# Residual of the late tokens turned by VectorE, and sums of their first norm taken along columns of a second copy of the input

## The chip, the cores and the metric

The kernel runs on one core of one Trainium2 chip. Its engines work side by side, each through its own queue, in order: TensorE (PE; its weight loads are shown apart as PEld), VectorE (DVE), ScalarE (ACT), GpSimd (POOL), and SyncE (SP), which only issues DMAs here. The time is that of the device in microseconds; for the kernel before it is the median of three runs. TensorE writes its results to PSUM, which has eight banks of 128 x 512 values; all other tiles lie in SBUF, 128 partitions wide.

## The reference

Two layers over 1024 tokens of 1024 features, float32: a retention layer with four heads, and a stick-breaking attention layer with eight heads whose keys and values come from the stream after the first layer. Each is normed before and after; `h` is the residual. Cut to what the change touches:

```python
def rms_norm(x, g):
    xf = x.astype(jnp.float32)
    y = xf * lax.rsqrt(jnp.mean(xf * xf, axis=-1, keepdims=True) + EPS)
    return (y * g.astype(jnp.float32)).astype(x.dtype)

h = x
u = rms_norm(h, ret_norm_pre[i])          # the first norm
proj = u @ ret_w_in[i]
...                                       # retention, gate, y = o @ ret_w_out[i]
h = h + rms_norm(y, ret_norm_post[i])     # the residual that is kept for the end
...                                       # shared keys and values, attention, gate
y = o @ sb_w_out[j]
h = h + rms_norm(y, sb_norm_post[j])      # the output
```

## The kernel before

Tokens are worked in two halves, 0 to 511 (early) and 512 to 1023 (late). Activations lie feature by feature: a tile has 128 features on the partitions and 512 tokens along the row, so the input is given transposed (`xT`). A float32 product is made of three faster ones: `split` (L511) writes each operand as a high part (ScalarE, L514, or L517 with a scale) and a low part (VectorE, L515 or L518), and `mm3` (L410) issues three matmuls, L413, L414 and L415. Weights come in loads of 256 KB (`wraw`) and are split into `whl`. Nearly all DMAs are issued by the helper at L360 on SP's queue.

**The first norm.** `a_open` has two halves. For the early tokens (`F`) the raw input is multiplied at once and scaled afterwards; its squares are added up by `squares` (ScalarE L557 and L560, VectorE L561), `rstd_col` sums over the partitions with four small matmuls against ones (L488), VectorE and GpSimd make the reciprocal root (L490, L492), `diag` spreads the column over a diagonal tile `sgn` (L499, L500), and `keep_row` broadcasts it with two matmuls (L506) into a row tile `acc` (ScalarE L508). `norm` (L588) then multiplies the input with that row and splits it into `xh` tiles. For the late tokens (`L`) `later` loads eight tiles of 128 x 512 into `v` and squares them in the same way, feature by feature; the same three steps (`stats1`) make their row, and `scale` (L605) applies it.

**The end.** The late tokens' output is made token by token: `finish` multiplies with the heads' outputs as the fixed operand, so that a tile has 128 tokens on the partitions. `prep` loads the last weights (`whl`, `ko`, `A`), the four tiles of residual `h` of 128 features-by-twos x 1024 (`xh`, 512 KB each) and the gain (`sgn`). Four blocks of 128 tokens follow; each has two or three pieces of twelve matmuls (`piece`, PSUM tags `ma` and `mb`), whose result VectorE adds up (L1387), ScalarE squares (L1388) and VectorE multiplies with the gain (L1393). The residual lies feature by feature, so `turn` (L1395) turns its 128 x 128 blocks with TensorE, eight for each block of tokens, into two PSUM tiles (`z` or `o`); `write` scales and adds it (L1406) and stores.

**What sets the order.** The program is written out step by step, with tables that hang steps onto chunks of matmuls (`at[j]`) and `merge` that spreads side steps over main ones. Then `arrange` (L101) plans anew: from a cost for each instruction and the dependencies it places every instruction of every engine, SP's DMAs among them, and fixes each queue's order. Tiles of one tag share a number of buffers (`BUFS`: `xh` 8, `ko` 2, `vo` 4, `wraw` 6, `whl` 3), and the plan keeps the order in which they are handed out.

Of the kernel before, what the change touches and what calls it, by code (L numbers as in the profile page):

```python
# [307 lines left out]
@with_exitstack  # L308
def trunk(ctx, tc, xT, wts, gains, trig, ident_in, cols, last_gain, out):

# [213 lines left out]
    turned = out[0:512, :].rearrange("a (b t) -> (a b) t", b=2)  # L524
    straight = out[512:1024, :]
    st_d = [[dr.tile([128, 512], F32, tag=f"st{h}{d}", name=f"st{h}{d}") for d in range(2)] for h in range(NH)]
    y_d = [[dr.tile([128, 512], F32, tag=f"y{t}{c}", name=f"y{t}{c}") for c in range(8)] for t in range(2)]
# [20 lines left out]
    def a_open():  # L548
# [26 lines left out]
        def stats(box):  # L575
            def stat1():
                box.col = rstd_col(box.acc)

            def stat2():
                box.d = diag(box.col)  # L580

            def stat3():
                box.row = keep_row(box.d)
            return [stat1, stat2, stat3]
# [9 lines left out]
        def later(k):  # L594
            i, c = k // 2, k % 2
            if c == 0:
                F.kept[i] = S("v", [2, 512])
            src = F.kept[i][:, c]
            dma(src, xT[128 * (i + 4 * c):128 * (i + 4 * c) + 128, HT:2 * HT])
            squares(L, src, k)  # L600

        def scale(kt):
# [4 lines left out]
        return F, [lambda k=k: load(k) for k in range(8)], stats(F), [lambda k=k: norm(k) for k in (0, 1, 2, 3, 4, 5, 6, 7)], \  # L607
            [lambda k=k: later(k) for k in range(8)], stats(L), scale

# [722 lines left out]
    def c_post(t, y_d, acc):  # L1332
# [23 lines left out]
        return [stat1, stat2, row] + in_turn(8, 1, load, add)  # L1356

    def finish(t, P, ys):

        w, hs, box = {}, [], {}  # L1360

        def prep(u):
# [7 lines left out]
            a = S("xh", [1024])  # L1370
            dma(a[:], h_d[t][u][:])
            hs.append(a)
# [21 lines left out]

        def turn(b):  # L1395
            box["h", b] = [PS("o" if b % 2 else "z") for _ in range(2)]
            for c in range(8):
                nc.tensor.transpose(box["h", b][c // 4][:, 128 * (c % 4):128 * (c % 4) + 128],
                                    hs[c // 2][:, 512 * (c % 2) + 128 * b:512 * (c % 2) + 128 * b + 128], ident[:])

        def write(b):
            r, y = S("col", [4]), box["y"]
            G.tensor_tensor(r[:, 0:1], box["s"][:, 3:4], mhalf[:, 0:1], ALU.pow)
            for nh in range(2):
                cl = slice(512 * nh, 512 * nh + 512)
                V.scalar_tensor_tensor(y[:, cl], y[:, cl], r[:, 0:1], box["h", b][nh][:], ALU.mult, ALU.add)  # L1406
                dma(straight[128 * b:128 * b + 128, cl], y[:, cl], nc.scalar if nh else nc.sync)

        def last():
            for b in range(4):  # L1410
                piece(b, 0, 0, 512)
                if b < 3:
                    turn(b)
                for k, a in ((1, 512),) if b < 3 else ((1, 512), (2, 768)):
                    piece(b, k, a, 512 if b < 3 else 256)
                if b == 3:
                    turn(b)
                write(b)
# [58 lines left out]
    def layer_a():  # L1477
# [27 lines left out]
        for j, k in zip((8, 8, 9, 9, 10, 10, 11, 11), range(8)):  # L1505
            at[j].append(later[k])
        for j, k in zip((12, 13, 14), range(3)):
            at[j].append(stats1[k])
# [43 lines left out]
    def layer_c(units, out, load, kept, post):  # L1552
# [38 lines left out]
        filler = P.pieces(end, halt)  # L1591
        merge(heads[0].mix(0), (filler[:3], 0, 1))
        merge(rows_of(1), (filler[3:6], 0, 0))
        merge(heads[0].mix(1), (filler[6:], 0, 1), (rows_of(2), 0, 1))
        ys, acc = [], []
        for n in range(2, 16):
            A = heads[n // 2]
            if n % 2 == 0:
# [4 lines left out]
                pre[0]()  # L1603
            extra = []
            if n == 9:
# [86 lines left out]
```

## Time and profile before

| | us |
|---|---|
| median of 3 runs (1628.98 to 1630.21) | 1629.36 |
| the profiled execution | 1628.69 |
| its span, first to last instruction | 1626.7 |
| TensorE busy | 1619.3 |
| VectorE busy | 1219.1 |
| ScalarE busy | 804.1 |
| GpSimd busy | 122.1 |
| mean DMA rate | 238 GB/s |

The profiled execution takes 1.99 us more than its span. Rows of a timeline read: start, duration, engine, line and operation, the tile written and the tiles read without their numbers, the shape, and in brackets how long the engine had been idle and what released it. The chain of waits is followed back from the last instruction; its rows are start, duration, engine, tile and line. A matmul row lasts longer than the step to the next, since matmuls are pipelined: the step between starts is what one costs. A matmul of 128 x 1 in full float32 appears as two rows.

### The profile page before, as it was taken

To read this page: it belongs to the slowest core of one execution; us is meant where nothing else is said; L and a number is where in the kernel's file an instruction comes from. 1 tells how busy PE (TensorE), PEld (TensorE's weight loads), DVE (VectorE), ACT (ScalarE), POOL (GpSimd) and SP (SyncE) were. 2 spreads that over 40 slices of the span, in tenths; PEclk is the share of its full clock that TensorE was granted. 3 is DMA by queue.
4 is the path that set the end of the run, shared out by engine and by line. 5 is a ranking of instruction groups with operands and counts; after the bars stand their busy time and mean duration, and the time that the engine had idled before them with its cause. 6 is when DMAs were issued, how large, how long until landed. Compare 5 with 4: busy or idle time off the path is not lost.

```text
span 1626.7 us, 22505 instructions
## 1 busy us (share of the span) xinstructions
PE 1619.3 (100%) x7659; PEld 1351.5 (83%) x7659; DVE 1219.1 (75%) x1956; ACT 804.1 (49%) x1535; POOL 122.1 (8%) x271
## 2 busy tenths in 40 slices
PE   9999999999999999999999999999999999999998
PEld 7888888888888888888888888888888888888887
DVE  8997866654668888887689877767658666878775
ACT  8553334433456555544356665566544433554432
POOL 0000000000022212211000000000001111010010
PEclk9999999999999999999999999999999999999999
DMA  9556765543377878784776788978337877869781
GB/s 319 188 175 252 247 211 189 208 141 133 112 267 254 308 246 285 234 290 146 242 278 223 260 312 290 344 278 308 119 126 259 314 279 259 282 214 331 253 272 52
DMA packets 175890, 386.43 MB, mean 238 GB/s; under 512 B 18080, under 2 KB 34592, under 8 KB 173216
## 3 DMA queue, kind: packets, MB, share of 16 engines
q1 hardware_dynamic: 175056, 383.93, 68.3%
q8 instruction: 60, 0.98, 0.2%
q10 hardware_dynamic: 720, 1.07, 0.2%
q14 instruction: 54, 0.44, 0.1%
HBM read 263.82 MB, written 121.11 MB: 237 GB/s over the span
## 4 chain that ended last, share of the span: by engine, by line
PE 98%; DMA 1%; DVE 0%; issue 0%; ACT 0%; SPq 0%; DVEq 0%; POOLq 0%; POOL 0%
PE pma L413 12%; PE pma L415 12%; PE pma L414 12%; PE pmb L413 9%; PE pmb L415 9%; PE pmb L414 9%; PE po L414 6%; PE po L415 6%; PE po L413 6%; PE pz L414 3%; PE pz L415 3%; PE pz L413 3%; PE pz L1298 2%; PE pz L770 1%; PE pz L488 0%; DMA wraw<-in_wts_dram 0%
## 5 line engine op out<-in xcount | busy, mean ns | idle before, releaser
L514 ACT ACTIVATE whl<-wraw 128x512 fp32r<-128x512 f32 x266 | 156.2, 625 | 175.1 <-issue 62.6
L515 DVE TENSOR_TENSOR whl<-wraw,whl 128x512 fp32r<-128x512 f32 x266 | 176.1, 686 | 87.0 <-ACT whl L514 84.4
L1270 DVE TENSOR_TENSOR_SCAN sgn<-sgn 128x128 f32<-128x128 f32 (+3 forms) x64 | 86.6, 1352 | 17.3 <-POOL sgn L1268 17.3
L515 DVE TENSOR_TENSOR AT<-pz,AT 128x512 fp32r<-128x512 f32 (+1 forms) x96 | 51.1, 551 | 50.0 <-ACT AT L514 49.6
L514 ACT ACTIVATE AT<-pz 128x512 fp32r<-128x512 f32 (+1 forms) x96 | 45.1, 492 | 68.4 <-PE pz L1298 67.9
L413 PE MATMUL pmb<-oT,whl 128*128 128x512 f32 x192 | 75.9, 395 | 0.0
L415 PE MATMUL pmb<-oT,whl 128*128 128x512 f32 x192 | 75.3, 392 | 0.0
L414 PE MATMUL pmb<-oT,whl 128*128 128x512 f32 x192 | 75.1, 391 | 0.0
L413 PE MATMUL pmb<-qk,whl 128*128 128x512 f32 x184 | 72.5, 394 | 0.0
L415 PE MATMUL pmb<-qk,whl 128*128 128x512 f32 x184 | 72.1, 392 | 0.0
L414 PE MATMUL pmb<-qk,whl 128*128 128x512 f32 x184 | 71.8, 390 | 0.0
L515 DVE TENSOR_TENSOR whl<-vo,whl 128x512 fp32r<-128x512 f32 x62 | 41.7, 689 | 35.1 <-ACT whl L514 34.8
L884 ACT ACTIVATE f<-pma 128x512 f32<-128x512 f32 x52 | 30.7, 595 | 49.7 <-PE pma L415 49.3
L514 ACT ACTIVATE whl<-vo 128x512 fp32r<-128x512 f32 x62 | 37.5, 624 | 34.7 <-PE pma L415 17.5
L413 PE MATMUL pma<-xh,whl 128*128 128x512 f32 x136 | 53.3, 392 | 0.0
L414 PE MATMUL pma<-xh,whl 128*128 128x512 f32 x136 | 53.1, 390 | 0.0
L415 PE MATMUL pma<-xh,whl 128*128 128x512 f32 x136 | 53.1, 390 | 0.0
L1267 POOL TENSOR_SCALAR_AFFINE_SELECT A<-A 128x128 f32<-128x128 f32 x32 | 10.8, 336 | 535.1 <-DMA ko<-k 395.4
L907 ACT ACTIVATE wraw<-wraw,gn 128x256 f32<-128x256 f32 x102 | 45.4, 497 | 7.9 <-DMA wraw<-in_wts_dram 7.9
L1262 ACT ACTIVATE xh<-pz 128x512 f32<-128x512 f32 (+3 forms) x48 | 23.6, 492 | 48.6 <-PE pz L415 48.4
L1263 ACT ACTIVATE sgn<-pz 128x512 f32<-128x512 f32 (+2 forms) x96 | 46.7, 488 | 0.0
L1262 ACT ACTIVATE A<-pz 128x512 f32<-128x512 f32 (+3 forms) x48 | 23.6, 491 | 42.5 <-PE pz L415 42.4
(580 smaller groups left out, 5137.0 us busy)
## 6 DMA issues: line engine op xcount, KB each, us to landing
wraw<-in_wts_dram SPq DMA_DIRECT2D x332, 256.0 KB, 3.8
whl<-w SPq DMA_DIRECT2D x56, 512.0 KB, 6.0
vo<-in_wts_dram SPq DMA_DIRECT2D x70, 256.0 KB, 4.4
xh<-k SPq DMA_DIRECT2D x32, 512.0 KB, 6.8
v<-v SPq DMA_DIRECT2D x32, 512.0 KB, 5.0
k<-A SPq DMA_DIRECT2D x21, 512.0 KB, 4.9
e<-whl SPq DMA_DIRECT2D x10, 1024.0 KB, 6.7
whl<-e SPq DMA_DIRECT2D x10, 1024.0 KB, 6.7
```

The source lines that it names most:

```text
L413: MM(p, lh, rh, start=start, stop=False, **kw)
L414: MM(p, lh, rl, start=False, stop=False, **kw)
L415: MM(p, ll, rh, start=False, stop=stop, **kw)
L514: A_.activation(dst[0], src, AF.Copy)
L515: V.tensor_tensor(dst[1], src, f32(dst[0]), ALU.subtract)
L770: nc.tensor.transpose(pt[:, 128 * e:128 * e + 128], on[:, 128 * e:128 * e + 128], ident[:])
L884: A_.activation(c[:], p[:], AF.Copy)
L907: A_.activation(x, x, AF.Copy, scale=gcol(self.gains[col], 2 * (2 * i + k) + c))
L1262: A_.activation(a[:, o:o + ww], p[:, :ww], AF.Sigmoid)
L1263: A_.activation(n[:, o:o + ww], p[:, :ww], AF.Sigmoid, scale=-1.0)
L1270: V.tensor_tensor_scan(n[:, :W][:, ::-1], n[:, :W][:, ::-1], n[:, :W][:, ::-1], 1.0, ALU.mult, ALU.bypass)
L1298: nc.tensor.transpose(p[:, 128 * tb:128 * tb + 128], self.A[hh][tb][:, c0:c0 + 128], ident[:])
```

## The change

It has two parts, and the places in the tables that they need.

The residual of the late tokens is turned ahead of time. Eight steps `turn_h`, spread over four stages of the attention layer, each load one 128 x 512 tile of `h` into `vo`, let VectorE turn its blocks of 32 x 32 in place in the tile (a block (i, j) stays at (i, j), its inside is turned), and store it to `ht` in DRAM. `prep` then gathers each block of 128 tokens with four loads of 32 partitions, each made of 32 x 32 runs of 32 values (128 bytes), into `xh`, now with tokens on the partitions. `turn` is gone, and `write` reads `xh` instead of PSUM.

The late tokens' sum of squares is taken along rows of a second copy of the input, `x_late`, with tokens on the partitions: four loads of 512 KB into `ko`, each squared by ScalarE with its running sum (`accum_out`), which gives the column that the four small matmuls gave. `later` still loads the eight feature tiles, for `scale`, but squares nothing.

```diff
@@ trunk
+    ht_d = dr.tile([1024, 512], F32, tag="ht", name="ht")
@@ a_open
         def stats(box):
             def stat1():
-                box.col = rstd_col(box.acc)
+                if box is F:
+                    box.col = rstd_col(box.acc)
+                    return
+                ms = S("small", [4])
+                V.tensor_scalar(ms[:], box.sum[:], 1.0 / D, EPS, ALU.mult, ALU.add)
+                box.col = S("col", [4])
+                G.tensor_tensor(box.col[:], ms[:], mhalf[:, 0:4], ALU.pow)
...
             dma(src, xT[128 * (i + 4 * c):128 * (i + 4 * c) + 128, HT:2 * HT])
-            squares(L, src, k)
+
+        def sums(i):
+            if i == 0:
+                L.sum = S("small", [4])
+            w = S("ko", [1024])
+            dma(w[:], x_late[128 * i:128 * i + 128, :])
+            A_.activation(w[:], w[:], AF.Square, accum_out=L.sum[:, i:i + 1])
...
-            [lambda k=k: later(k) for k in range(8)], stats(L), scale
+            [lambda k=k: later(k) for k in range(8)], [lambda i=i: sums(i) for i in range(4)] + stats(L), scale
@@ before finish
+    def turn_h(k):
+        a, x = S("vo", [512]), S("vo", [512])
+        dma(a[:], h_d[1][k // 2][:, 512 * (k % 2):512 * (k % 2) + 512])
+        V.transpose(x[:], a[:])
+        dma(ht_d[128 * k:128 * k + 128, :], x[:])
+
@@ finish, prep
             a = S("xh", [1024])
-            dma(a[:], h_d[t][u][:])
+            for j in range(4):
+                dma(a[32 * j:32 * j + 32, :].rearrange("a (k b) -> a k b", b=32),
+                    ht_d[:].rearrange("(k a) t -> a k t", a=32)[:, :, 128 * u + 32 * j:128 * u + 32 * j + 32])
@@ finish
-        def turn(b):
-            box["h", b] = [PS("o" if b % 2 else "z") for _ in range(2)]
-            for c in range(8):
-                nc.tensor.transpose(box["h", b][c // 4][:, 128 * (c % 4):128 * (c % 4) + 128],
-                                    hs[c // 2][:, 512 * (c % 2) + 128 * b:512 * (c % 2) + 128 * b + 128], ident[:])
...
-                V.scalar_tensor_tensor(y[:, cl], y[:, cl], r[:, 0:1], box["h", b][nh][:], ALU.mult, ALU.add)
+                V.scalar_tensor_tensor(y[:, cl], y[:, cl], r[:, 0:1], hs[b][:, cl], ALU.mult, ALU.add)
...
-                if b < 3:
-                    turn(b)
...
-                if b == 3:
-                    turn(b)
@@ layer_a
-        for j, k in zip((12, 13, 14), range(3)):
+        for j, k in zip((11, 12, 13, 13, 14, 15, 15), range(7)):
             at[j].append(stats1[k])
@@ layer_c
-        merge(heads[0].mix(0), (filler[:3], 0, 1))
-        merge(rows_of(1), (filler[3:6], 0, 0))
+        merge(heads[0].mix(0), (filler[:2], 0, 1))
+        merge(rows_of(1), (filler[2:6], 0, 0))
...
-            extra = []
+            extra = [lambda k=k: turn_h(k) for k in (2 * n - 4, 2 * n - 3)] if 2 <= n < 6 else []
@@ inputs
+        "x_late": np.ascontiguousarray(x[0, HT:]),
```

The plan moves instructions; a number behind a name tells buffers apart and differs between the two programs. Lines from 580 on are some dozen higher in the changed kernel (L588 becomes L595, L1406 becomes L1421).

TensorE, the first block of the end, before (`qk` holds the last heads' outputs, `ko` and `A` the last weights):

```order
L413 MATMUL pma_15391<-ko_15293,qk_15160 128x512
L414 MATMUL pma_15391<-ko_15293,qk_15160 128x512
L415 MATMUL pma_15391<-ko_15293,qk_15160 128x512
L1398 MATMUL pz_15409<-ident,xh_15254 128x128 x2
L1398 MATMUL pz_15409<-ident,xh_15296 128x128 x2
L1398 MATMUL pz_15410<-ident,xh_15341 128x128 x2
L1398 MATMUL pz_15410<-ident,xh_15375 128x128 x2
L413 MATMUL pma_15419<-A_15335,qk_15160 128x512
L414 MATMUL pma_15419<-A_15335,qk_15160 128x512
```

and now:

```order
L413 MATMUL pma_15429<-ko_15322,qk_15186 128x512
L414 MATMUL pma_15429<-ko_15322,qk_15186 128x512
L415 MATMUL pma_15429<-ko_15322,qk_15186 128x512
L413 MATMUL pma_15447<-A_15367,qk_15186 128x512
L414 MATMUL pma_15447<-A_15367,qk_15186 128x512
L415 MATMUL pma_15447<-A_15367,qk_15186 128x512
```

The eight turnings between the first and the second piece are gone; the pieces follow each other.

VectorE in the opening, around the last parts of the early tokens' diagonal (`sgn`), before:

```order
L499 TENSOR_SCALAR sgn_541<-ident,col_518 128x128
L500 SCALAR_TENSOR_TENSOR sgn_541<-ident,col_518,sgn_541 128x128
L515 TENSOR_TENSOR whl_648<-wraw_649,whl_648 128x512
L1150 TENSOR_TENSOR small_601<-col_518,cc 128x1
L1150 TENSOR_TENSOR small_612<-col_518,cc 128x1
L1150 TENSOR_TENSOR small_623<-col_518,cc 128x1
L515 TENSOR_TENSOR whl_648<-wraw_653,whl_648 128x512
L1150 TENSOR_TENSOR small_634<-col_518,cc 128x1
L588 SCALAR_TENSOR_TENSOR A_368<-A_368,gn,acc_565 128x512
```

and now:

```order
L499 TENSOR_SCALAR sgn_542<-ident,col_519 128x128
L515 TENSOR_TENSOR whl_649<-wraw_650,whl_649 128x512
L500 SCALAR_TENSOR_TENSOR sgn_542<-ident,col_519,sgn_542 128x128
L1163 TENSOR_TENSOR small_602<-col_519,cc 128x1
L1163 TENSOR_TENSOR small_613<-col_519,cc 128x1
L1163 TENSOR_TENSOR small_624<-col_519,cc 128x1
L1163 TENSOR_TENSOR small_635<-col_519,cc 128x1
L515 TENSOR_TENSOR whl_649<-wraw_654,whl_649 128x512
L595 SCALAR_TENSOR_TENSOR A_369<-A_369,gn,acc_566 128x512
```

A weight split has moved ahead of the last L500; on TensorE the second of the two L506 matmuls that read the diagonal has moved two matmuls back.

SP's queue ahead of the end, before (`w` are the last weights in DRAM):

```order
L360 DMA ko_15293<-w_229 128x2x256
L360 DMA ko_15293<-w_231 128x2x256
L360 DMA xh_15254<-h_104 128x1024
L360 DMA xh_15296<-h_105 128x1024
L360 DMA whl_15249<-w_228 128x2x256
L360 DMA whl_15249<-w_230 128x2x256
```

and the stretch now from the same weights on:

```order
L360 DMA whl_15275<-w_231 128x2x256
L360 DMA xh_15280<-ht 32x32x32
L360 DMA xh_15373<-ht 32x32x32
L360 DMA xh_15410<-ht 32x32x32
L360 DMA xh_15325<-ht 32x32x32
L360 DMA xh_15280<-ht 32x32x32
L360 DMA ko_15322<-w_232 128x2x256
L360 DMA xh_15373<-ht 32x32x32
L360 DMA sgn_15415<-in_last_gain_dram 128x1024
L360 DMA xh_15325<-ht 32x32x32
L360 DMA xh_15280<-ht 32x32x32
```

One residual load has become four, and the second `ko` load and the gain stand among them: two of the sixteen come ahead of the `whl` loads, five more ahead of that `ko` load.

More of the change, by code (lines that the diff above doesn't have):

```diff
@@ L308, in trunk @@
 @with_exitstack
-def trunk(ctx, tc, xT, wts, gains, trig, ident_in, cols, last_gain, out):
+def trunk(ctx, tc, xT, wts, gains, trig, ident_in, cols, last_gain, x_late, out):
     nc = tc.nc
```

## The prediction

> **What bounds the kernel now.** I read the chain of waits first, then the busy times by stretch, then the timeline of TensorE at the places that the change touches.
>
> ```profile
> PE 98%; DMA 1%; DVE 0%; issue 0%; ACT 0%; SPq 0%; DVEq 0%; POOLq 0%; POOL 0%
> ```
> ```profile
> 1.71:1621.42 1619.71, 1619.25 (x7659) 1351.46 (x7659) 1216.60 (x1950) 803.66 (x1535) 121.27 (x266) 1.00 0.69 238
> ```
>
> The first is the page's chain that ended last: TensorE is 98% of it. The second is the stretch from TensorE's first to its last instruction; its columns are the stretch, its length, then busy time of TensorE, its weight loads, VectorE, ScalarE and GpSimd, granted clock, DMA share, GB/s. TensorE is busy 1619.25 of 1619.71 us at the full clock. So the kernel gets faster only by what leaves TensorE's queue ahead of its last matmul, and slower by any wait that comes into it. VectorE, ScalarE and the DMAs have room on average; what matters is where they are late.
>
> **What leaves TensorE.** The first turning of residual tiles, on TensorE's timeline (start, duration, engine, line):
>
> ```profile
> 1597.07 0.39 PE L413 MATMUL pma<-ko,qk 128*128 128x512 f32 x1
> ...
> 1598.20 0.40 PE L415 MATMUL pma<-ko,qk 128*128 128x512 f32 x1
> 1598.44 1.04 PE L1398 MATMUL pz<-ident,xh 128*128 128x128 f32 x8
> 1599.23 0.48 PE L413 MATMUL pma<-A,qk 128*128 128x512 f32 x1
> 1599.54 0.40 PE L414 MATMUL pma<-A,qk 128*128 128x512 f32 x1
> ```
>
> Matmuls of this size start every 0.226 us (five steps from 1597.07 to 1598.20). From the L415 at 1598.20 to the L414 at 1599.54 are two steps, 0.45, but 1.34 us pass: eight turnings cost 0.89. The chain shows all of them that lie on it:
>
> ```profile
> 1598.60 0.87 PE pz L1398 x8
> ...
> 1604.94 0.87 PE po L1398 x8
> ...
> 1611.30 0.44 PE pz L1398 x4
> ```
>
> Twenty of the 32 turnings are there: 0.87 + 0.87 + 0.44 = 2.18, and with the slower restart seen above 0.89 + 0.89 + 0.46 = **2.24 us**. The other twelve come after the last matmul:
>
> ```profile
> 1619.82 0.28 PE L415 MATMUL pma<-A,qk 128*128 128x256 f32 x1
> ...
> 1620.38 1.04 PE L1398 MATMUL po<-ident,xh 128*128 128x128 f32 x8
> ...
> 1621.54 0.65 POOL L1403 TENSOR_TENSOR col<-small,mhalf 128x1 f32<-128x1 f32 x1 [4.68 <-DVE small L1392]
> 1622.23 1.41 DVE L1406 SCALAR_TENSOR_TENSOR AT<-AT,col,po 128x512 f32<-128x512 f32 x2 [0.44 <-POOL col L1403]
> ```
>
> They end at 1621.42, and what VectorE's last sums wait for is GpSimd's power, done at 1622.19. Taking these twelve away brings nothing; the tail behind the last matmul stays as it is (its sums now read SBUF instead of PSUM; I leave them at 1.41).
>
> The sum of squares of the late tokens, in the chain of the opening:
>
> ```profile
> 44.06 0.79 PE pz L488 x8
> 44.84 0.35 PE pma L413
> ```
>
> 0.79 for the four small matmuls (each shown twice), and the next one takes 0.35 instead of 0.23: **0.91 us**. The sums now come out of ScalarE as columns. Together 2.24 + 0.91 = 3.15 us leave TensorE.
>
> **What it adds at the opening.** On ScalarE eight squares of 128x512 become four of 128x1024; on VectorE seven sums go away. Both engines have less to do or the same, but the order around the first broadcast (L506, which the first split of the normed tiles waits for) changes. VectorE, then ScalarE, then TensorE:
>
> ```profile
> 23.88 0.35 DVE L500 SCALAR_TENSOR_TENSOR sgn<-ident,col,sgn 128x128 fp32r<-128x128 f32 x1
> 24.55 0.69 DVE L515 TENSOR_TENSOR whl<-wraw,whl 128x512 fp32r<-128x512 f32 x1 [0.31 <-ACT whl L514]
> ...
> 31.91 1.29 DVE L515 TENSOR_TENSOR xh<-A,xh 128x512 fp32r<-128x512 f32 x2
> ```
> ```profile
> 24.94 1.14 ACT L560 ACTIVATE f<-v 128x512 f32<-128x512 f32 x2
> 25.98 0.58 ACT L508 ACTIVATE acc<-pz 128x512 f32<-128x512 f32 x1
> ```
> ```profile
> 25.27 0.62 PE L506 MATMUL pz<-sgn,onesr 128*128 128x512 f32 x2
> ...
> 31.39 0.39 PE L415 MATMUL pmb<-whl,xh 128*128 128x512 f32 x1
> 31.76 0.50 PE L413 MATMUL pma<-whl,xh 128*128 128x512 f32 x1
> 32.10 0.40 PE L414 MATMUL pma<-whl,xh 128*128 128x512 f32 x1
> 32.66 0.50 PE L415 MATMUL pma<-whl,xh 128*128 128x512 f32 x1 [0.16 <-DVE xh L515]
> ```
>
> TensorE already waits here for the splits that VectorE begins at 31.91: 1.27 us pass in three steps that take 0.68, a loss of 0.59, about 0.7 with the slow step behind it (0.34 instead of 0.226, as at 31.76). By the new order the split at 24.55, which waits for ScalarE, stands ahead of the last L500. That L500 then starts near 25.16 and ends near 25.5, and the second L506 matmul is issued two places later than before: 25.95 instead of 25.50. ScalarE's L508 follows it at 26.4 instead of 25.98. The first big square, put between 24.94 and L508, costs about what the two old squares there cost (1.14), so it is done by 26.1 and does not decide. From L508 on VectorE's order up to the xh splits is the one of before, so they come 0.42 later, and so does the L415 at 32.66: **+0.42 us**. Bounds: -0.7 if something makes up for all of it and the old wait goes too, +1.0 if a weight split or a late load adds as much again. I take 0.42, since it follows from rows that keep their order.
>
> The second copy of the late input is 2 MB more (four loads of 512 KB), and DMA is full in the opening. In the new order two of the four stand ahead of the eleventh load of weights (split at 24.55), but half of the old 256 KB loads of late tokens have moved behind it, so it has the same bytes ahead of it, the next 0.26 MB more. From the sixteenth to the eighteenth load of weights it is 0.5 to 1.6 MB more. The loads in the first row here are the fifteenth to the seventeenth, the splits in the second those of the fifteenth and sixteenth:
>
> ```profile
> 24.33 1.96 SPq L360 DMA_DIRECT2D wraw<-in_wts_dram  x3
> ```
> ```profile
> 38.43 1.16 ACT L514 ACTIVATE whl<-wraw 128x512 fp32r<-128x512 f32 x2 [2.69 <-PE pmb L415]
> ```
>
> Twelve us lie between the last issue and the splits, and 1.6 MB at the 2.26 MB in 6.2 us of a full queue (its row is below) are 4.4. I cost them at nothing; without that cover they would fall under the +1.0.
>
> **What it adds in the attention layer.** Eight times: a load of 256 KB, a VectorE turning of 128x512 in blocks of 32x32, a store of 256 KB. No row shows such a turning; the subtraction of two 128x512 tiles, 0.69 above, is the nearest, so some 5.5 us of VectorE, with half or twice that as bounds. The stretch where they lie reads, in one of its windows:
>
> ```profile
> 1260.00:1280.00 20.00, 20.00 (x112) 17.46 (x112) 12.92 (x24) 8.96 (x23) 3.92 (x12) 1.00 0.85 297
> ```
>
> VectorE is busy 12.92 of 20 us and TensorE never waits. Eight turnings over 100 us are hidden there. The 4.2 MB more at this row's 297 GB/s are 14 us of DMA time spread over that stretch, which has 0.15 free in this window: hidden, but not by much.
>
> **What it adds at the end.** Each of the four 512 KB loads of residual becomes four loads of 1024 runs of 128 bytes. No row has runs of 128 bytes in such a number. The lower bound is the load of the gains, 128 packets of 160 bytes alone on its queue in the first 4 us; the upper, a stretch of packets of which 1871 of 2094 are under 2 KB, 6.2 us long (queue, packets, MB, share of 16 engines):
>
> ```profile
> q10 hardware_dynamic: 144, 0.02, 3.0%
> ```
> ```profile
> q1 hardware_dynamic: 2094, 2.26, 102.1%
> ```
>
> 3.0% of 16 x 4 us over 144 packets is 13 ns a packet; 102.1% of 16 x 6.2 over 2094 is 48 ns. A load of 1024 runs is 64 packets on each engine: 0.85 us by the one, 3.1 by the other. I take the first, as 160 bytes is nearest. When must they be there?
>
> ```profile
> 1571.58 1.07 SPq L360 DMA_DIRECT2D xh<-h  x2
> ```
> ```profile
> out_dram<-AT SPq DMA_DIRECT2D x4, 256.0 KB, 2.0
> ```
>
> The first is issued near 1571.6. With 13 ns all sixteen take 13.6 us, the loads among them about 5.3 (five of weights with 256 packets, 0.77 each at 48 ns, and the gain's 512 KB, 1.4 at that stretch's 2.26 MB in 6.2 us), the landing 2.0 (shortest on the page): the last is there at 1592.5. The tile of the last block is read at 1622.2 less what was saved, 1619.5; the `ko` load, now behind seven of the sixteen, lands near 1583 for the matmul at 1597.07. I cost this at **nothing**; the 27 us between 1592.5 and 1619.5 are the cover.
>
> [...]
>
> **The sum.** -2.24 - 0.91 + 0.42 = -2.73. The profiled execution took 1628.69 (span 1626.7, 1.99 around it): it would take 1625.96. It lies 0.67 below the median 1629.36, so the median goes to **1626.6 us**, 0.17% less.
>
> **The rivals.**
> 1. The opening gains instead of losing: with seven sums fewer on VectorE the xh splits come in time. -3.15 - 0.7 = -3.85: 1625.5. For it: VectorE has no idle time there before. Against: all seven sums stand behind the splits that TensorE waits for.
> 2. The plan is made anew, and TensorE's order differs at several places of the attention layer, with 4.2 MB more on the queue. If such waits as the opening's 0.7 come at three places, 2.1 of the gain go: 1628.7. For it: DMA shares of 0.85 and more there. Against: under the old plan, made by the same rules, TensorE was idle 0.46 of 1619.71 us.
> 3. Slower: the 128-byte loads end too late. At p ns a packet sixteen take 1.024 p us; the last block is late from 1571.6 + 1.024 p + 7.3 > 1619.5, so p above 40 ns. At 48 the tile is there at 1628.1, 5.9 later than VectorE's last sums began before: 1635. For it: runs at a stride of 2 KB in memory, which no row shows. Against: 13 ns for 160 bytes.
>
> **How the numbers follow.** The forecast has 0.52, the better opening 0.16, the waits of the attention layer 0.20, the slow loads 0.09, anything else 0.03. What a measurement here can tell from no change is about 0.2%, 3.3 us: below 1626.1 is faster. The better opening and a fifth of the forecast make faster 0.27; the slow loads and a little of the waits make slower 0.11; within 0.2% has 0.62. The forecast's own range is 1626.0 to 1627.3; the range from 1625.3 to 1630.2 takes in the better opening and nearly all of the waits and leaves out the slow loads.
>
> **What would show it.** Right: no L1398 rows between the last matmuls and steps of 0.226 through them; no second L488; the L415 near 32.7 starting near 33.1; the last load of residual landing before 1600; TensorE's end about 2.7 earlier and a tail of the same length. Wrong: waits of TensorE between 1200 and 1600, a VectorE L1421 that waits for a DMA, or an opening in which TensorE no longer waits.

## The result, and the profile after

| | before | after |
|---|---|---|
| median of 21 runs each, us | 1630.32 (1628.98 to 1631.91) | 1627.30 (1626.50 to 1629.25) |
| profiled execution, us (span) | 1628.69 (1626.7) | 1627.26 (1625.3) |
| TensorE busy, us | 1619.3 | 1615.8 |
| DMA, MB | 386.43 | 392.72 |

The ratio of the runs is 0.9983, with a 95% interval of 0.9977 to 0.9989: the changed kernel is 0.17% faster, 3.0 us between the medians. The forecast was 1626.6 us, a step of -2.73.

The two profiled executions differ by 1.43 us only, half of what the medians do. Why is told with the experiments; first the places that the prediction named.

The chain of waits and the stretch from TensorE's first to its last instruction (columns as in the prediction), then the window of the attention layer:

```profile
PE 98%; DVE 1%; issue 0%; ACT 0%; DMA 0%; SPq 0%; DVEq 0%; POOLq 0%; POOL 0%
```
```profile
1.71:1618.72 1617.01, 1615.84 (x7619) 1348.08 (x7619) 1216.99 (x1946) 803.15 (x1533) 123.42 (x266) 1.00 0.71 242
1260.00:1280.00 20.00, 20.00 (x109) 17.27 (x108) 13.62 (x25) 8.61 (x23) 4.17 (x12) 1.00 0.96 345
```

TensorE still is the whole chain. Its idle time rose from 0.46 us to 1.17, nearly all of it ahead of 35 us: 0.67 ahead of 20 us, where one execution differs from the next (0.26 in the kernel before, 0.27 when the changed kernel was run again), and 0.47 of the rest at the place in the opening that the prediction named. In the attention layer VectorE has the turnings on top (12.92 to 13.62 us in the window) and the DMAs a share of 0.96 instead of 0.85, and TensorE is still busy for 20.00 of 20 us. All eight turnings together, as the trace groups them by line (duration min/median/max in ns):

```profile
L1374 DVE STREAM_TRANSPOSE vo<-vo x8: 700/704/706, 1232.6 to 1356.9; 128x512 f32<-128x512 f32 x8
```

The end, on TensorE's timeline, where eight turnings stood before between these two matmuls, and the last matmul; then GpSimd's power and VectorE's last sums:

```profile
1599.14 0.39 PE L415 MATMUL pma<-ko,qk 128*128 128x512 f32 x1
1599.36 0.39 PE L413 MATMUL pma<-A,qk 128*128 128x512 f32 x1
...
1618.44 0.28 PE L415 MATMUL pma<-A,qk 128*128 128x256 f32 x1
```
```profile
1620.17 0.54 POOL L1418 TENSOR_TENSOR col<-small,mhalf 128x1 f32<-128x1 f32 x1 [4.69 <-DVE small L1413]
```
```profile
1620.75 1.42 DVE L1421 SCALAR_TENSOR_TENSOR AT<-AT,col,xh 128x512 f32<-128x512 f32 x2 [0.66 <-POOL col L1418]
```

The step is 0.22 now. From the last matmul's start to the last two sums are 2.31 us, 2.41 before; the sums take 1.42 from SBUF and took 1.41 from PSUM.

The opening, VectorE, then TensorE, then ScalarE:

```profile
26.06 0.69 DVE L515 TENSOR_TENSOR whl<-wraw,whl 128x512 fp32r<-128x512 f32 x1 [0.68 <-ACT whl L514]
26.67 0.34 DVE L500 SCALAR_TENSOR_TENSOR sgn<-ident,col,sgn 128x128 fp32r<-128x128 f32 x1
```
```profile
26.78 0.39 PE L506 MATMUL pz<-sgn,onesr 128*128 128x512 f32 x1
...
27.46 0.39 PE L506 MATMUL pz<-sgn,onesr 128*128 128x512 f32 x1
...
34.49 0.50 PE L415 MATMUL pma<-whl,xh 128*128 128x512 f32 x1 [0.38 <-DVE xh L515]
```
```profile
26.45 1.05 ACT L613 ACTIVATE ko<-ko 128x1024 f32<-128x1024 f32 x1
27.40 0.18 ACT L613 ACTIVATION_READ_ACCUMULATOR ko<-ko 128x1 f32 x1
27.89 0.60 ACT L508 ACTIVATE acc<-pz 128x512 f32<-128x512 f32 x1 [0.30 <-PE pz L506]
```

The split at 26.06 waits 0.68 us for ScalarE with the last L500 queued behind it, the pair of L506 is torn apart by two matmuls, and TensorE's wait before the L415 grew from 0.16 to 0.38 us of idle time, as forecast. VectorE behind it, before and after, from the first product with the broadcast row to the first low part of xh:

```profile
26.59 0.75 DVE L588 SCALAR_TENSOR_TENSOR A<-A,gn,acc 128x512 f32<-128x512 f32 x1 [0.47 <-ACT acc L508]
...
28.67 0.68 DVE L515 TENSOR_TENSOR xh<-A,xh 128x512 fp32r<-128x512 f32 x1
```
```profile
28.52 0.75 DVE L595 SCALAR_TENSOR_TENSOR A<-A,gn,acc 128x512 f32<-128x512 f32 x1 [0.63 <-ACT acc L508]
...
30.51 0.68 DVE L515 TENSOR_TENSOR xh<-A,xh 128x512 fp32r<-128x512 f32 x1
```

The gathering loads, on SyncE's queue, and the DMA queue in a stretch that holds nothing but them (packets, MB, share of 16 engines):

```profile
1571.86 1.20 SPq L360 DMA_DIRECT2D xh<-ht  x2
...
1583.66 8.68 SPq L360 DMA_DIRECT2D xh<-ht  x8
```
```profile
q1 hardware_dynamic: 4298, 0.55, 88.3%
```

The stretch is 1588 to 1592: 88.3% of 16 x 4 us over 4298 packets is 13.1 ns a packet. The last load is issued from 1591.8 to 1592.3 and lands 2.8 us after its issue began: it is in place near 1594.6.

### The profile page after: what moved, and what is told of

Same layout as the page of the kernel before. It is cut to its first block, busy times and chain, and to the rows that moved or that the text cites. A ratio compares the mean times of both kernels' runs of the same rounds, so it can differ in the third digit from the quotient of the medians.

```text
span 1625.3 us, 22472 instructions
## 1 busy us (share of the span) xinstructions
PE 1615.8 (99%) x7619; PEld 1348.1 (83%) x7619; DVE 1220.5 (75%) x1957; ACT 804.1 (49%) x1535; POOL 124.2 (8%) x271
## 2 busy tenths in 40 slices
DMA packets 194834, 392.72 MB, mean 242 GB/s; under 512 B 34976, under 2 KB 51488, under 8 KB 192160
## 4 chain that ended last, share of the span: by engine, by line
PE 98%; DVE 1%; issue 0%; ACT 0%; DMA 0%; SPq 0%; DVEq 0%; POOLq 0%; POOL 0%
PE pma L413 12%; PE pma L414 12%; PE pma L415 12%; PE pmb L413 9%; PE pmb L414 9%; PE pmb L415 9%; PE po L414 6%; PE po L415 6%; PE po L413 6%; PE pz L415 3%; PE pz L414 3%; PE pz L413 3%; PE pz L1311 2%; PE pz L783 1%; DMA A<-in_xT_dram 0%
## 5 line engine op out<-in xcount | busy, mean ns | idle before, releaser
L415 PE MATMUL pmb<-oT,whl 128*128 128x512 f32 x192 | 75.3, 392 | 0.0
L414 PE MATMUL pmb<-oT,whl 128*128 128x512 f32 x192 | 75.2, 392 | 0.0
L415 PE MATMUL pmb<-qk,whl 128*128 128x512 f32 x184 | 72.2, 392 | 0.0
L414 PE MATMUL pmb<-qk,whl 128*128 128x512 f32 x184 | 71.8, 390 | 0.0
L897 ACT ACTIVATE f<-pma 128x512 f32<-128x512 f32 x52 | 30.8, 595 | 49.8 <-PE pma L415 49.4
L415 PE MATMUL pma<-xh,whl 128*128 128x512 f32 x136 | 53.1, 390 | 0.0
L414 PE MATMUL pma<-xh,whl 128*128 128x512 f32 x136 | 53.1, 390 | 0.0
L690 POOL TENSOR_SCALAR_AFFINE_SELECT sc<-sc 128x256 fp32r<-128x256 f32 x16 | 10.8, 692 | 447.6 <-DVE sc L515 447.4
```

The source lines that it names most:

```text
L414: MM(p, lh, rl, start=False, stop=False, **kw)
L415: MM(p, ll, rh, start=False, stop=stop, **kw)
L897: A_.activation(c[:], p[:], AF.Copy)
```

## The experiments

Single executions of this kernel differ by more than the terms in question, so the runs are read in two ways: by their medians, and by the trace, with the start of a matmul in a run against the same matmul in the first profile of the kernel before. The difference grows or shrinks where the kernels differ. It is taken at the starts that stand at 23.91, 33.22, 72.50, 849.9, 1598.20 and 1619.82 us in the kernel before; two of these rows, there and in the changed kernel:

```profile
72.50 0.39 PE L413 MATMUL pz<-whl,xh 128*128 128x512 f32 x1
```
```profile
73.39 0.39 PE L413 MATMUL pz<-whl,xh 128*128 128x512 f32 x1
```

0.89 at this place, and 0.94 from 1598.20 to 1599.14. The table has the growth in each stretch, in us:

| run | to 24 | 24 to 33, the opening | 33 to 72, L488 | 72 to 850 | 850 to 1598 | 1598 to the last matmul |
|---|---|---|---|---|---|---|
| changed kernel | +1.51 | +0.33 | -0.95 | -0.04 | +0.09 | -2.32 |
| changed kernel again | +0.13 | +0.33 | -0.95 | +0.35 | -0.11 | -2.32 |
| kernel before again | +0.78 | +0.01 | -0.01 | -0.01 | -0.21 | -0.04 |
| turned residual alone | +1.17 | +0.01 | -0.01 | +0.44 | +0.34 | -2.32 |
| sums of the second copy alone | +0.28 | +0.32 | -0.94 | +0.54 | -0.23 | 0.00 |
| no turnings behind the last matmul | +0.39 | +0.01 | -0.01 | +0.56 | -0.26 | 0.00 |
| the pair of L506 together | +3.13 | +0.01 | -0.96 | +1.27 | -0.02 | -2.32 |
| L508 ahead of the first big square | +0.86 | +0.15 | -0.97 | +0.31 | -0.04 | -2.32 |
| two big squares later | +1.57 | 0.00 | +0.85 | +0.30 | +0.08 | -2.32 |
| runs of 64 bytes | +1.52 | +0.33 | -0.95 | +0.56 | -0.11 | -2.32 |
| runs of 32 bytes | +2.69 | +0.34 | -0.93 | +0.05 | +0.04 | -2.32 |

Three columns, the opening, L488 and the end, repeat to a few hundredths in every kernel that has the edit, save where a run's own edit is made to move them, and are nil in every kernel that has not. The three others change from execution to execution of one and the same kernel: by up to 1.4 us up to 24, by 0.4 from 72 to 850, and by 0.2 from 850 to 1598.

**One part alone.** The kernel before with the residual part of the diff and nothing of the norm's:

```diff
+    ht_d = dr.tile([1024, 512], F32, tag="ht", name="ht")
...
+    def turn_h(k):
...
-            dma(a[:], h_d[t][u][:])
+            for j in range(4):
+                dma(a[32 * j:32 * j + 32, :].rearrange("a (k b) -> a k b", b=32),
+                    ht_d[:].rearrange("(k a) t -> a k t", a=32)[:, :, 128 * u + 32 * j:128 * u + 32 * j + 32])
...
-                if b < 3:
-                    turn(b)
...
+            extra = [lambda k=k: turn_h(k) for k in (2 * n - 4, 2 * n - 3)] if 2 <= n < 6 else []
```

> The kernel before with the turned residual alone: the eight turn_h, the gathering loads, no turnings on TensorE; the first norm's sums stay as before. By the theory of the sum only what stands ahead of TensorE's last matmul counts: 0.89 + 0.89 + 0.46 = -2.24 us at the end and nothing in the opening, so about 1628.1 where the kernel before has 1630.3. Its L415 near 32.7 us then stands against its first matmul as in the kernel before, and TensorE has no wait between 1200 and 1600 us. If the twelve turnings behind the last matmul counted too, the gain would be 3.6; if the 4.2 MB more of transfers made new waits in the attention layer, it would be 1 or less; if nearly all of the measured gain of 3 us came from the opening, it would be near 0.

Measured: 1627.28 against 1630.21, ratio 0.9983 (0.9975 to 0.9992). By the medians that is 2.9 us, more than the 2.24 expected and as much as the whole change; the trace has -2.32 at the end, nothing in the opening. The 4.2 MB of added transfers make no wait of TensorE that repeats: this trace has one of 0.15 us, for a load of `k` at 1260.4, and no other trace has one in that stretch. The +0.34 between 850 and 1598 stands beside -0.11 and +0.09 for the two profiles of the changed kernel, which has the same transfers. The eight profiles with the transfers have 0.03 there on average, the four without them -0.18; whether up to 0.2 us of that is their price, the runs do not tell.

The other part alone, the kernel before with the norm's part of the diff:

```diff
...
-            squares(L, src, k)
+        def sums(i):
...
+            dma(w[:], x_late[128 * i:128 * i + 128, :])
+            A_.activation(w[:], w[:], AF.Square, accum_out=L.sum[:, i:i + 1])
...
```

> The kernel before with the late sums taken along columns of the second copy of the input alone; the residual is still turned by TensorE. The theory: four small matmuls less, -0.91 us, and the L506 pair torn apart by the new order of VectorE, about +0.3 to +0.4, so -0.5 to -0.6 us in all. If the opening gained by its shorter VectorE work, -1.2 or more; if the 2 MB more of loads in the opening hold up weights, 0 or slower.

Measured: 1629.23 against 1630.21, ratio 0.9993 (0.9984 to 1.0002). By the medians that is no more than a hint; the trace has +0.32 and -0.94, together -0.62. The medians of the two parts add up to more than the whole. The time holds more than the span, and that part differs: of the 67 executions of the kernel before whose spans are on record, 17 took 2.2 to 3.2 us on top of the span, and of 32 of the changed kernel none took over 2.1. By the spans alone the medians fall by 2.4 us for the turned residual (1627.7 to 1625.3), by 0.4 for the sums (to 1627.3) and by 3.0 for both, in the second set of runs of the changed kernel (1627.7 to 1624.7); its first set, with no spans of the kernel before beside it, has 1625.3. That is near the -2.32, -0.62 and -2.94 of the trace. Medians of spans scatter as well, by some 0.6 here, so the sizes are the trace's.

**The twelve turnings that were costed at nothing.** The kernel before with a part of `turn` and `write` changed; it leaves the twelve turnings out and adds those parts of the residual unturned, so its output is not that of the reference:

```diff
-            for c in range(8):
+            for c in range((8, 8, 4, 0)[b]):
...
-                V.scalar_tensor_tensor(y[:, cl], y[:, cl], r[:, 0:1], box["h", b][nh][:], ALU.mult, ALU.add)
+                V.scalar_tensor_tensor(y[:, cl], y[:, cl], r[:, 0:1], (box["h", b][nh] if 2 * b + nh < 5 else hs[b][:, cl])[:], ALU.mult, ALU.add)
```

> The kernel before without the twelve turnings that stand behind its last matmul: the residual of the last block and of the second half of the third is added as it lies in SBUF, unturned, so those outputs are other numbers. The first twenty turnings stay. The theory costs these twelve at nothing, since VectorE's last sums wait for GpSimd's power and not for them: 1630.3 as the kernel before, within 0.2 in the trace. If a turning counted wherever it stands, 1.3 us would go.

Measured: 1629.72 against 1629.63, ratio 1.0002 (0.9993 to 1.0012), and 0.00 in the trace up to the last matmul. The last two sums start 2.31 us after the start of that matmul instead of 2.41, as in the changed kernel; that is all the twelve bring.

**The opening's loss.** The changed kernel with two steps moved in the finished plan, VectorE's last L500 behind its L499 and TensorE's second L506 behind the first:

```diff
-    order = best[1]
+    order = ahead_of(best[1], steps, users, tags)
...
+    first = users[tags["sgn"][0]]
+    dve = [s.k for s in first if s.eng == "DVE"]
+    pe = [s.k for s in first if s.eng == "PE"]
+    d, p = order["DVE"], order["PE"]
+    d.remove(dve[-1])
+    d.insert(d.index(dve[-2]) + 1, dve[-1])
+    p.remove(pe[1])
+    p.insert(p.index(pe[0]) + 1, pe[1])
```

> The changed kernel with two instructions put back where they stood before the change: VectorE's last L500 ahead of the weight split that waits for ScalarE, and TensorE's second L506 right behind the first. All else is the order of the changed kernel. If the torn pair is what costs the opening its 0.31 us, the second L506 starts 0.45 earlier, ScalarE's L508 then follows the first big square at once, about 0.3 earlier, and TensorE's wait before the L415 for the split of xh shrinks by 0.3: 1627.0 instead of 1627.3. If the big square ahead of L508 or a late weight is the cause, nothing moves.

Measured: 1626.55 against 1630.21, ratio 0.9980 (0.9971 to 0.9989). The median is 0.75 below the changed kernel's, but the intervals overlap; the trace tells the place: +0.01 instead of +0.33. On VectorE, ScalarE and TensorE:

```profile
25.46 0.35 DVE L500 SCALAR_TENSOR_TENSOR sgn<-ident,col,sgn 128x128 fp32r<-128x128 f32 x1
```
```profile
28.07 1.04 ACT L613 ACTIVATE ko<-ko 128x1024 f32<-128x1024 f32 x1
...
29.11 0.57 ACT L508 ACTIVATE acc<-pz 128x512 f32<-128x512 f32 x1
```
```profile
35.79 0.50 PE L415 MATMUL pma<-whl,xh 128*128 128x512 f32 x1 [0.17 <-DVE xh L515]
```

L508 no longer waits for TensorE, it follows the big square at once, and the wait before the L415 is back to 0.17, against 0.16 in the kernel before. So the late L500 with the torn pair of L506 is the cause of the 0.33; the two were put back together and not each by itself. It is also the limit of this edit: now the square is what L508 stands behind. Next, both L506 three places earlier and L508 ahead of that square (`q` is ScalarE's queue, `j` the place of L508):

```diff
-    p.remove(pe[1])
-    p.insert(p.index(pe[0]) + 1, pe[1])
+    i = p.index(pe[0]) - 3
+    for k in pe:
+        p.remove(k)
+    p[i:i] = pe
...
+    q[j - 1], q[j] = q[j], q[j - 1]
```

> As the one with the two instructions put back, and further: both L506 three places earlier and ScalarE's L508 ahead of the first big square. If the broadcast row is what the xh splits wait for, the row is there about 1 us earlier, VectorE's first L595 starts where the weight split ahead of it ends, about 0.6 earlier, and the wait of TensorE for xh (0.38 idle, some 0.8 with the slow steps round it) goes: 0.6 to 0.8 us less than the changed kernel, about 1626.6. If VectorE's own work between the row and the splits sets the wait, no more than the 0.3 of the smaller edit.

Measured: 1627.30 against 1630.21, ratio 0.9981 (0.9973 to 0.9990). The broadcast row is there earlier, but the opening still loses 0.15, a gain of 0.18 on the changed kernel where 0.6 to 0.8 was expected:

```profile
26.10 0.60 ACT L508 ACTIVATE acc<-pz 128x512 f32<-128x512 f32 x1 [0.21 <-PE pz L506]
26.59 1.06 ACT L613 ACTIVATE ko<-ko 128x1024 f32<-128x1024 f32 x1
```
```profile
28.34 0.75 DVE L518 SCALAR_TENSOR_TENSOR sc<-pma,small,sc 128x512 fp32r<-128x512 f32 x1 [0.71 <-ACT sc L517]
```

The big square now stands ahead of ScalarE's L517, and VectorE, with its first L595 done early, waits 0.71 us for that. The row was not what the xh splits hung on alone; the wait moved one step on. So, in that order, the squares themselves were moved, the first behind the L517 and the second behind three copies of xh (`big` are the squares in ScalarE's queue):

```diff
+    q.remove(big[0])
+    q.insert(q.index(big[1]), big[0])
+    q.remove(big[1])
+    q.insert(q.index(big[2]), big[1])
```

> As the one with L508 ahead of the first big square, where VectorE then stood idle 0.71 us for ScalarE's L517, with the first big square moved behind the four L517 and the second behind the three xh copies. If the squares on ScalarE are what holds VectorE's chain, its first L518 starts 0.7 earlier (near 27.6 against a TensorE start as there), the second xh split ends near 32.8 instead of 33.6 and TensorE's wait before the L415 goes: 0.6 to 0.8 us less than with the order of that run, about 1 us less than the changed kernel. If the later release of the ko tiles, on which SyncE waits for the third and fourth load of the second copy with weight loads behind it, makes weights late, a new wait of TensorE between 35 and 60 us takes it back.

Measured: 1627.96 against 1629.79, ratio 0.9988 (0.9979 to 0.9997). The opening comes out at 0.00, a gain of 0.33 on the changed kernel where about 1 was expected, and the next stretch takes back 1.8:

```profile
28.17 0.69 ACT L517 ACTIVATE sc<-pma,small 128x512 fp32r<-128x512 f32 x1 [0.76 <-PE pma L415]
...
41.74 1.06 ACT L613 ACTIVATE ko<-ko 128x1024 f32<-128x1024 f32 x1 [2.68 <-DMA ko<-in_x_late_dram]
```
```profile
44.95 0.50 PE L413 MATMUL pma<-whl,xh 128*128 128x512 f32 x1 [0.56 <-ACT sg L897]
```

With the squares out of the way ScalarE's first L517 waits 0.76 us for TensorE, and VectorE's first L518 still 0.54 for that L517: the squares were not all that held it. Behind that, the ko tiles come free later, the last load of the second copy comes later, ScalarE waits 2.68 us for it, and the L897 behind it frees TensorE's bank late. The squares are better left where the changed kernel has them. Of the versions tried, the one with the L506 together has the least in the trace, 0.32 below the changed kernel; the medians do not tell these two apart.

**The gathering loads.** How far are they from being late? Twice the loads, in runs of 64 bytes, and four times, in runs of 32 (8 in the place of each 16 of the diff):

```diff
-            for j in range(4):
-                dma(a[32 * j:32 * j + 32, :].rearrange("a (k b) -> a k b", b=32),
-                    ht_d[:].rearrange("(k a) t -> a k t", a=32)[:, :, 128 * u + 32 * j:128 * u + 32 * j + 32])
+            for j in range(0, 128, 16):
+                dma(a[j // 32 * 32:j // 32 * 32 + 32, :].rearrange("a (k b) -> a k b", b=32)[:, :, j % 32:j % 32 + 16],
+                    ht_d[:].rearrange("(k a) t -> a k t", a=32)[:, :, 128 * u + j:128 * u + j + 16])
```

> The changed kernel with the residual gathered by 32 loads in runs of 64 bytes instead of 16 in runs of 128: the same bytes, twice the packets and twice the issues. At about 1.05 us for a load back to back, as the changed kernel's eight last ones show, the 32 take 33.6 us from 1571.9, with 7 us of other loads and the landing the last is there near 1613. If, as forecast, only the last block's deadline of 1619.5 counts, the time stays as it is (1627.3 within 0.7). If the first block's is the deadline (VectorE reads its tile at 1604.65, and its sums for the following pieces stand behind it in the queue, so the PSUM banks stay full), VectorE waits there up to 8 us and the end comes 2 to 5 us later.

> The changed kernel with 64 loads in runs of 32 bytes: four times the packets and issues for the same bytes. At 1.05 us a load the last is there near 1646. By the deadline of the last block the end comes 27 us later (1654); with VectorE's queue held at the first block, TensorE stops when its four banks are full and has some 7 us of matmuls left when the tiles come: 30 to 35 us later. If the price went by bytes and not by packets and issues, nothing would change.

Measured: 1627.67 and 1637.88 us, one execution each. SyncE's queue with 64 bytes, the queue's packets between 1590 and 1602, then SyncE's and VectorE's rows with 32 bytes:

```profile
1586.53 16.99 SPq L360 DMA_DIRECT2D xh<-ht  x22
```
```profile
q1 hardware_dynamic: 17546, 1.11, 99.0%
```
```profile
1583.38 41.74 SPq L360 DMA_DIRECT2D xh<-ht  x58
```
```profile
1625.50 4.06 DVE L1421 SCALAR_TENSOR_TENSOR AT<-AT,col,xh 128x512 f32<-128x512 f32 x6 [4.23 <-DMA xh<-ht]
...
1632.01 0.75 DVE L1421 SCALAR_TENSOR_TENSOR AT<-AT,col,xh 128x512 f32<-128x512 f32 x1
```

With 64 bytes nothing is late: the last load is issued by 1603.5 and lands near 1605.7, and the first block's sums, which this run's plan puts behind the add of one more piece, begin at 1606.0. 99.0% of 16 x 12 us over 17546 packets is 10.8 ns each. A load takes 0.77 us of the queue, not the 1.05 that both theories used, and 0.72 with 32 bytes, so both numbers expected of the last run were too late by far: the first block's tile is whole at 1625.4, the last load lands at 1627.1, and the end comes 9.3 us later against the last matmul (1632.76 less 1622.17, less the 1.24 by which the last matmul is late). The deadline is real, then, and it is the end that pays. The first block did not hold VectorE's queue either way, since the plan, made anew with the added loads, puts all eight L1421 behind the adds of all pieces with 32 bytes; TensorE never stops (its matmuls of 512 columns start every 0.23 us from 1597.66 to 1616.70). Whether an unchanged plan would have stopped it was not tried.

**Execution against execution.** Both kernels once more, unaltered:

> The changed kernel once more, unaltered, beside the other on the same chip. If the 1.5 us that its first profile lost before 17.4 us against the profile before belong to the execution (TensorE's half rate at the start, and loads), another execution of the same kernel shows another loss there, between 0 and 2 us, while the steps of the change stay: about -0.9 at the L488, -2.27 at the end, +0.3 in the opening. If they belong to the change, the loss is 1.5 again, within 0.1.

> The kernel before once more, unaltered, for one more profile: if its first profile was an execution with a fast start, this one shows TensorE's half rate lasting past 5.3 us and a span nearer the median (about 1628.3 where the first had 1626.7); if that start is its own, the matmuls stand within 0.1 us of the first profile up to 17 us.

Measured: the changed kernel 1626.67 against 1629.79 us, ratio 0.9981 (0.9973 to 0.9990), its profile with a span of 1624.1; the kernel before 1629.11 in its one execution, span 1627.2 where about 1628.3 was expected. The starts of the same matmuls of the first weights, in the second profile of the changed kernel, in its first and in the second of the kernel before:

```profile
5.72 0.58 PE L413 MATMUL pma<-whl,oT 128*128 128x512 f32 x1
6.14 0.40 PE L414 MATMUL pma<-whl,oT 128*128 128x512 f32 x1
6.38 0.40 PE L415 MATMUL pma<-whl,oT 128*128 128x512 f32 x1
```
```profile
5.72 0.63 PE L413 MATMUL pma<-whl,oT 128*128 128x512 f32 x1
6.15 0.63 PE L414 MATMUL pma<-whl,oT 128*128 128x512 f32 x1
6.57 0.63 PE L415 MATMUL pma<-whl,oT 128*128 128x512 f32 x1
...
7.43 0.56 PE L414 MATMUL pma<-whl,oT 128*128 128x512 f32 x1
7.82 0.40 PE L415 MATMUL pma<-whl,oT 128*128 128x512 f32 x1
```
```profile
5.72 0.63 PE L413 MATMUL pma<-whl,oT 128*128 128x512 f32 x1
6.15 0.63 PE L414 MATMUL pma<-whl,oT 128*128 128x512 f32 x1
6.58 0.46 PE L415 MATMUL pma<-whl,oT 128*128 128x512 f32 x1
```

Where a step is 0.43, TensorE runs at half its later rate of 0.23. That ends near 6.1 us in the first of the three, near 7.8 in the second (the step from 7.43 to 7.82 is still 0.39) and near 6.7 in the third; in the first profile of the kernel before it ended ahead of 5.5. With what waits follow up to 24 us it makes 0 to 1.6 us, whatever the kernel, leaving aside the two runs of the last section. So the 1.51 of the changed kernel's first profile belongs to the execution: another one has 0.13, and its span is 2.6 below that of the first profile of the kernel before. Nor does the order leave room for the change there: TensorE's is the same in both kernels up to 25 us and ScalarE's up to 17.4, and the second copy's first load is issued at 12.48 us. In the changed kernel's first profile ScalarE waits for an early load of the input,

```profile
7.96 0.72 ACT L517 ACTIVATE oT<-A,gn 128x512 fp32r<-128x512 f32 x1 [1.97 <-DMA A<-in_xT_dram]
```

and works without a pause from there to the L897 that TensorE waits for at 18.12.

## Why the prediction was right

The steps, each with its term and what the traces have in its place:

| step | forecast | measured |
|---|---|---|
| twenty turnings ahead of the last matmul | -2.24 | -2.32 |
| twelve behind it | 0 | 0.00 at the last matmul, -0.1 at the last sums, under 0.05 at the end of the span |
| four sums of squares, L488 | -0.91 | -0.95 |
| the opening, last L500 and second L506 late | +0.42 | +0.33 |
| the attention layer | 0 | -0.3 to +0.3, in kernels with and without the transfers |
| sixteen loads of 128-byte runs | 0 | 0 |
| sum, to the last matmul | -2.73 | -2.94 (medians: -3.0, again -3.1) |

- **TensorE's queue.** The twenty turnings alone account for nearly all, -2.32 in all eight runs without them, 0.00 or -0.04 in the three that have them. That a turning counts only ahead of the last matmul is shown by the kernel without the twelve.
- **The opening.** The mechanism stood as put: the split waits for ScalarE (the idle time was 0.68 and not 0.31: before, the L500 filled 0.35 of it), the L500 behind it comes late, the second L506 two matmuls later, L508 after it. Putting the pair together gives the loss back to 0.01. VectorE's first product with the row starts 0.42 later, as put (28.52, less the 1.51 that this execution had lost before, against 26.59). The size at the L415 was 0.09 too high, since VectorE is quicker from there to the first low part of xh, 1.99 us instead of 2.08. The first big square stands ahead of L508, which could not have started before its end at 27.58, and started at 27.89. That the square does not decide, as the prediction had it, holds for the changed kernel and stops holding 0.3 us further on.
- **Turnings on VectorE.** 0.70 us each, 0.69 taken from the subtraction; hidden.
- **The loads.** 13.1 ns a packet where 13 was taken and 48 was the upper bound. But a load takes 1.09 us of SyncE's queue (8.68 for eight), not 0.85, and the last lands near 1594.6, not 1592.5: the term was mis-sized by 2 us inside a cover of 10. The prediction measured its cover of 27 up to the last block; the first block's sums, at 1604.65, are the nearer deadline. The slow loads of the third rival did not come, but its mechanism is real: four times the packets, with the same bytes, put the last load at 1627.1 and the end 9.3 us later.
- **The waits of the attention layer**, the second rival, did not come: TensorE is busy for 20.00 of 20 us at a DMA share of 0.96. The better opening, the first rival, did not come either.
- **Against the profile or against the medians.** The prediction worked its sum against one profiled execution, 1628.69, and carried over its distance to the median of three runs, 1629.36. That execution had the fastest start of all twelve profiles, and the median of 21 runs lies at 1630.32. By the same step from there the forecast would have been 1627.6; the measured 1627.3 lies between the two. That it lies within the forecast's own range, at its upper end, is in part luck: the base was 0.96 too low and the step 0.3 too small, and the two errors go against each other. The medians' -3.0 beside the trace's -2.94 is also closer than it should be, by the time outside the span that is told with the two parts. And the prediction took 0.2% as what runs can tell from no change; with 21 runs each the interval is 0.06% to either side, and 0.17% is told. The single profile of the changed kernel had a slow start, and two profiles alone would have shown half of the gain.

## What to carry to other kernels

On a kernel with one engine busy from end to end, list what leaves that engine's queue ahead of its last instruction, and cost the same operation behind that point at nothing: here the same turning was worth 0.11 us or none by its place. When a plan is made anew, look for pairs that it tears apart and for a wait that stands ahead of something short and urgent; moving two instructions back gave 0.3 us, moving the next ones only passed the wait on. And when two profiles differ by no more than two of one kernel do (here up to 1.4 us from the start alone), align the same instructions and read the difference stretch by stretch, with one more profile of each kernel, before any of it is put down to the change.

## What was not expected

**TensorE falls to half rate in the middle of the opening, in some executions.** In the run with the pair of L506 together, the start cost 3.13 us, only 1.56 of it up to the L414 at 18.95 (17.39 in the kernel before). First TensorE's rows of that run, then its stretch from 19.5 to 24 us and the part of it at half rate, and last the stretch of the kernel before (columns as above; the clock is the third number from the end):

```profile
18.15 0.50 PE L413 MATMUL pma<-whl,qk 128*128 128x512 f32 x1 [0.60 <-ACT sg L897]
18.95 0.50 PE L414 MATMUL pma<-whl,qk 128*128 128x512 f32 x1 [0.30 <-DVE whl L515]
...
21.00 0.63 PE L415 MATMUL pma<-whl,qk 128*128 128x512 f32 x1
21.42 0.63 PE L413 MATMUL pmb<-whl,qk 128*128 128x512 f32 x1
```
```profile
19.50:24.00 4.50, 4.50 (x19) 3.65 (x18) 3.74 (x10) 4.21 (x9) 1.40 (x1) 0.64 0.88 295
20.75:24.17 3.42, 3.42 (x9) 2.65 (x9) 3.11 (x9) 3.12 (x6) 1.40 (x1) 0.50 0.89 274
```
```profile
19.50:24.00 4.50, 4.50 (x21) 3.67 (x21) 4.12 (x12) 4.25 (x9) 1.32 (x1) 1.00 1.04 340
```

The granted clock is 0.64 over the stretch and 0.50 in the part from 20.75 to 24.17, where the steps are 0.42 and 0.43 us; in the kernel before they are 0.23 there, at a clock of 1.00. The half rate follows two waits of 0.60 and 0.30 us and the eight small L488. The run with 32 bytes has the like: its granted clock is 0.50 from 20.5 to 23.5. The other ten profiles have no such stretch: they lose 1.57 us at most up to 24 us, where these two lose 3.13 and 2.69. The first of the changed kernel has waits of 0.37 and 0.30 us at the same two matmuls and the same L488, and goes on in steps of 0.23, so waits of nearly that length do not bring it by themselves. In the 3.42 us ahead of the half rate five matmuls of 512 columns start (18.15 to 20.57); where TensorE does not wait, 15 do. What brings it on is not shown: no run moved it on purpose. The stretch at half rate cost this run 1.6 us (3.13 less 1.56). Six of the 32 executions of the changed kernel have a mean granted clock of 0.998, as the run above has, and took 1.4 to 2.5 us more than the median of the others; of the 67 of the kernel before two have it. That these fell to half rate at the same place, and more often by the change, is not shown. In the first 6 us the profile's granted clock reads 1.00 although the steps are 0.43.

**Short runs hardly differ in price.** 13.1 ns a packet for 128 bytes, 10.8 for 64, from DRAM at a stride of 2 KB. A load of 1024 runs took 1.09, 0.77 and 0.72 us of SyncE's queue with 128, 64 and 32 bytes a run: from 64 to 32 bytes a load saved 0.05 us.
